# A mixture-of-experts decoder layer on one core: gate and branch products with the tokens on the partitions, merged rows transposed, and 24 unread products in the routing

## The chip, the cores and the metric

The kernel runs on one core of a Trainium2 chip. The time is device microseconds of one execution. Before the change three runs gave 510.54, 511.18 and 512.19 us, with a median of 511.18 us.

## The reference

One layer of a decoder works on 256 tokens of width 1024, all in float32. It has two halves, and a layer norm with a residual closes each. The core of it is:

```
p  = split(x @ w_in)                                   # q, k, v, ... of four mixers, and 4 x 1024 gate columns
ys = stack(mixer_a, mixer_b, mixer_c, mixer_d)         # each (256 tokens, 256)
gates  = sigmoid(p["gate"].reshape(256, 4, 1024))
merged = sum_n gates[:, n] * (ys[:, n] @ w_branch[n])  # (256, 1024)
x = layer_norm(ALPHA * x + merged @ w_out)
# routing: one of 4 groups, then 2 of its 8 experts for each token; then
y = sum over the chosen experts of weight * down(silu(gate(x)) * up(x))
x = layer_norm(ALPHA * x + y)
```

The mixers are A (dilated sliding-window attention), B (attention to the 64 best keys of an indexer), C (chunked gated linear attention) and D (a delta-rule recurrence). There are 32 experts with three matrices of 1 MB each, 96 MB of weights in all.

## The kernel before

**Precision.** Products of the first half are made of three fp32r products: an operand is split into a high part (ScalarE, `A.copy`, line 366) and a low part (VectorE, line 367), and `mm3` (lines 379 to 383) issues low times high, high times low and high times high into one PSUM bank.

**The tiles of w_in.** `TILES` lists 56 tiles of 128x1024 numbers: 24 for the mixers, then for each branch, in the order B, A, C, D, eight gate tiles `gB0` to `gB7` and so on. `gen_S` splits a tile and issues the loads of later ones; `gen_P` makes the products of a tile. A gate tile holds 128 gate columns for all 1024 inputs. Its weights are the stationary operand and the 256 tokens of x the moving one, so that a tile is 8 x 3 products of 256 columns; two tiles fill one of the two PSUM banks of the pool `pj`, and one tanh (line 489) empties it.

**Merging.** `gen_M` does sixteen steps, four to a branch. A step makes 12 products of 256 columns (the branch weights are stationary, the branch's tokens move), then VectorE multiplies by one plus the tanh (line 1182), and from the second branch on GpSimd, or VectorE for the last branch D, adds (line 1185). For D the sum is split into high and low (lines 1192 and 1194). The result lies with the model dimension on the partitions. `gen_N` loads and splits the branch weights, and `gen_U` loads x and splits the output weights. `gen_O` makes merged @ w_out: 96 products of 512 columns, of which the first 48 need only the first half of the merged rows, and the next 48 the second half.

**Routing.** `gen_R(0)` and `gen_R(1)` do a token half each: residual, transposes (line 1367), router logits (line 1384), then a row of small VectorE steps, products with `tri` and `ones` for the ranks (lines 1415 and 1417), and the selection matrix. `gen_E` gathers the tokens of the first four experts (line 1464). `gen_Z` normalises.

**Experts.** Eight groups of four experts follow. `gen_L` starts to fetch their weights once the mixers' memory is given back (`gen_X`); up to 25 pieces of 1 MB are ahead, and each later piece is issued on SP's queue (line 1264) when the products that read its slot are done. 17 slots of the pool `rp` are shared by all that lasts long: loaded and split tiles, gates, merged rows, and the pieces of expert weights.

**The order.** All of this is Python generators, and each `yield` ends a step. The string `ORDER` names, letter by letter, which generator does its next step, so it fixes the order of the instructions on every engine and in SP's queue. Each engine works through its own in order.

Of the kernel before, what the change touches and what calls it, by code (L numbers as in the profile page):

```python
# [9 lines left out]
F32 = mybir.dt.float32  # L10
# [7 lines left out]
P = 128  # L18
# [95 lines left out]
def _layout(inp):  # L114
# [14 lines left out]
    for n in TILES:  # L129
        if n[:2] in ("av", "cv"):  # L130
            o0 = (512 if n[0] == "a" else 1640)
            h = int(n[2])
            cols.append(W[512 * h:512 * h + 512, o0:o0 + 256].reshape(4, P, 256).transpose(1, 0, 2).reshape(P, 1024))
            continue
        if n == "sm":
            c = sm
        elif n == "ck":
            c = ck
        else:
            o0 = 3000 + 1024 * "ABCD".index(n[1]) + 128 * int(n[2]) if n[0] == "g" else at[n[:-1]] + 128 * int(n[-1])  # L140
            c = W[:, o0:o0 + 128]
        cols.append(c.reshape(KT, P, P).transpose(1, 0, 2).reshape(P, 1024))
    o["win"] = np.stack(cols).reshape(len(TILES) // 2, 2, P, 1024).transpose(0, 2, 1, 3)
# [65 lines left out]
SA = 1  # L209

ORDER = (
    "PSBYNDSSFSUSSXSSDPRSSQZPCDOSPEPDDDBSDDDDSPDPPDSDPDDSDPDSPPPFSDFPSPDWAFDDPPDPBSDDPDSDDBBDDDPFDDDDDPDP"
    "SDSWDPDPDBBPPWDSDSBPBBDPDSDBDPCSCDCPBPDDDWDBBMCDDBDDDBWSDSPPBWDDBBSBPDBBDPDDBWDDDDDSDDBDBDBDDBDPBDDP"
    "DBBPDDDSPDDDBDDSPDPBDDDDBDSPDDDDDBDDDDDPNNBNBDDPDDDDDDDDBPAADAANAAAADSDDDDDAASADPPAABDDABABADPBBSAAB"
    "BADADAADDDBBDBAAAAADDBDSDDBDDBBDBBPASBBBBSBBBBDPDBDPBBBCDCPBCCBBBAPSMCMCDCCCCMNCCCPCMCCMSCCCCPPSPPMN"
    "MSPNSMNPSMPSMMPMNCCSPMPSCPDDSPPPCMSSNPMCMSMMLCXPSMLLLLMPLNLNPSMMPSPLPSMMPSMMMPPSNPSPMPSPNSMMLMPPSMMM"
    "PMNPMMLNMPSMSMPMMPMSUUUUUPUMMMMMPPOUULOLLUOSULPMMLMLUUMOLOUUOUUUUOQLOQQQQQQQQQOLLQQQLQQQYYUQQRLQORRQ"
    "RLRRRRQRRRQRRZRQZQERRRRRRRRRLLLREEQQERRE"
)


def body(ctx, tc, I, out):
# [90 lines left out]
    wpart(1, 1)  # L313
    SY.dma_start(pc, I["pc"])
    SY.dma_start(lw, I["lw"])
    load_tiles(2)
    SY.dma_start(cst[:, 0:CC["m2"][0]], I["cst"][:, 0:CC["m2"][0]])
    SY.dma_start(csts, I["cst"][:, NMIX:NCC])
    SY.dma_start(cst[:, CC["m2"][0]:NMIX], I["cst"][:, CC["m2"][0]:NMIX])
    for i in range(4, AHEAD, 2):  # L320
# [108 lines left out]
    def gen_S():  # L429

        yield 0
        first = [(*twin("hl", [P, KT, P], dt=F32R), view(w_sb.pop(i), 1024, [P, KT, P])) for i in range(2)]
        for c in "x0 w00 x1 x2 w01 x3 w10 w11".split():
            if c[0] == "x":
                ks = slice(2 * int(c[1]), 2 * int(c[1]) + 2)
                halves(xh[:, ks], xl[:, ks], xT[:, ks])
            else:
                i, ks = int(c[1]), slice(4 * int(c[2]), 4 * int(c[2]) + 4)
                hi, lo, src = first[i]
                halves(hi[:, ks], lo[:, ks], src[:, ks])  # L440
                sp[i] = hi, lo
            if c in ("x3", "w11"):
                parts["S"] += 1
            yield 0
        nxt = AHEAD
        for i, n in enumerate(TILES):
            if i > 1:
                sh = [P, 4, 256] if n[:2] in ("av", "cv") else [P, KT, P]
                sp[i] = split(view(w_sb.pop(i), 1024, sh), sh)
                parts["S"] = i + 1  # L450
            while nxt < len(TILES) + KT and nxt < i + 1 + (AHEAD if i < 8 else MID if i < TI["av1"] else NEAR):
                if nxt < len(TILES):
                    load_tiles(nxt)
                else:
                    load_out()
                nxt += 2

            yield ("P", i - SA)

    def gen_P():  # L460
        pair = None
        for i, n in enumerate(TILES):
            if n in ("av0", "cv0"):
                continue
            yield ("S", i + 1)
            if n in ("av1", "cv1"):
                p = ps([P, 2, 256], pj)
                for q in range(2):
                    for k in range(KT):
                        h, l = sp[i - 1 + k // 4]  # L470
                        mm3(p[:, q], xp(k, slice(128 * q, 128 * q + 128)), (h[:, k % 4], l[:, k % 4]), k == 0, k == KT - 1)
                yield 0
                evacuate(n, p)
                parts["P"] = i + 1
                continue
            c = int(n[-1]) % 2 if n[-1].isdigit() else 0
            if c == 0:
                pair = ps([P, 2, S], pj)
            h, l = sp.pop(i)
            for k in range(KT):  # L480
                mm3(pair[:, c], (h[:, k], l[:, k]), xp(k), k == 0, k == KT - 1)
            if n[0] == "g":
                m = int(n[2])
                if c:
                    yield 0
                    if m == 1:
                        gslot[n[1]] = slot("g" + n[1], [P, 4, 2, S])
                    gts[n[1], m // 2] = t = gslot[n[1]][:, m // 2]
                    A.activation(t, pair, AF.Tanh, scale=0.5)
                    if i == len(TILES) - 1:  # L490
                        ready(AF.Sqrt, t[:, 1, 0:1])
            else:
                if i == 0:
                    V.tensor_scalar(omm, pc[:, PC["mu"][0]:PC["mu"][0] + 7], -1.0, 1.0, op0=OP.mult, op1=OP.add)
                if n == "ak0":
                    G.memset(into("ak", [P, 2, 2, S]), 0.0)
                yield 0
                evacuate(n, pair[:, c])
            parts["P"] = i + 1


# [658 lines left out]
    def gen_M():  # L1160
        parts["M"] = 0
        for b_, n in enumerate(ORDER_OF_BRANCHES):
            first, final = b_ == 0, b_ == 3
            for jj in range(4):
                i, j2 = jj // 2, slice(2 * (jj % 2), 2 * (jj % 2) + 2)
                yield (n, ("N", 2 * b_ + i + 1))
                h, l = wsp[2 * b_ + i]
                yh, yl = parts[n]
                pbr = ps([P, 2, S])
                for c in range(2):  # L1170
                    cs = slice(256 * (jj % 2) + 128 * c, 256 * (jj % 2) + 128 * c + 128)
                    for k in range(2):
                        mm3(pbr[:, c], (h[:, k, cs], l[:, k, cs]), (yh[:, k], yl[:, k]), k == 0, k == 1)
                parts["M"] += 1
                yield TI[f"g{n}{2 * jj + 1}"] + 1
                g = gts.pop((n, jj))
                if first and jj % 2 == 0:
                    if i == 0:
                        t = slot("mg", [P, 2, 4, S])
                        mg.extend((t[:, 0], t[:, 1]))  # L1180
                dst = mg[i][:, j2]
                V.scalar_tensor_tensor(f2(dst) if first else f2(g), in0=f2(g), scalar=1.0, in1=f2(pbr), op0=OP.add, op1=OP.mult)
                if not first:
                    yield 0
                    (V if final else G).tensor_tensor(dst, dst, g, op=OP.add)
                if final:
                    yield 0
                    if jj == 0:
                        for m in range(2):
                            t = slot("mg" + "hl"[m], [P, 2, 4, S], dt=F32R)  # L1190
                            mgs[m].extend((t[:, 0], t[:, 1]))
                    A.copy(mgs[0][i][:, j2], dst)
                    yield 0
                    V.tensor_tensor(mgs[1][i][:, j2], dst, mgs[0][i][:, j2].bitcast(F32), op=OP.subtract)
                    if jj % 2:
                        parts["mg%d" % i] = True

    def gen_W():

# [144 lines left out]
    def gen_R(q):  # L1344
# [11 lines left out]
        for h in range(2):  # L1356
# [22 lines left out]
                parts["rs%d" % q] = (mv[:, 0:1], rs)  # L1379
            yield 0  # L1380
            if h == 0:
                pl = ps([P, 36])
            for k in range(4 * h, 4 * h + 4):
                T.matmul(pl, lhsT=zT[:, k], rhs=gw[:, k], start=k == 0, stop=k == KT - 1)
        yield 0
        lg = sq_([P, 36], "lg", bufs=2)
        V.scalar_tensor_tensor(lg, in0=pl, scalar=rs, in1=bw, op0=OP.mult, op1=OP.add)

        sm = sq_([P, 8], "smr", bufs=2)
        gm, fm, sg, w1, nv, ex = (sm[:, i:i + 1] for i in range(6))  # L1390
# [20 lines left out]
        V.tensor_scalar(oh[q], le2[:, 0:32], -4.0 * BIG, None, op0=OP.is_equal)  # L1411
        yield "sel0" if q else 0
        if q == 0:
            prks.extend(ps([P, 32]) for _ in range(2))
        T.matmul(prks[q], lhsT=C("tri"), rhs=oh[q], start=q == 0, stop=True)
        if q == 0:
            T.matmul(prks[1], lhsT=C("ones"), rhs=oh[0], start=True, stop=False)
        prk = prks[q]
        yield 0

        rank[q] = sq_([P, 32], "rank%d" % q)
# [52 lines left out]

    XG = {}

    def gen_E():
        yield ("sel0", "nrm0")
        pg = []
# [7 lines left out]
        for kh in range(2):  # L1487
# [3 lines left out]

    gens = {"S": gen_S(), "P": gen_P(), "F": gen_F(), "D": gen_D(), "B": gen_B(), "C": gen_C(), "A": gen_A(), "N": gen_N(),
            "M": gen_M(), "W": gen_W(), "X": gen_X(), "L": gen_L(), "U": gen_U(), "O": gen_O(), "Q": gen_R(0), "R": gen_R(1),
            "Y": gen_Z(0), "Z": gen_Z(1), "E": gen_E()}
    for g in ORDER:
        next(gens[g], None)
    assert all(next(g, None) is None for g in gens.values())
# [283 lines left out]
```

## Time and profile before

| | us |
|---|---|
| profiled execution, its own time | 511.06 |
| span of its instructions | 509.3 |
| TensorE busy | 465.8 (91%) |
| VectorE busy | 239.1 (47%) |
| ScalarE busy | 195.2 (38%) |
| GpSimd busy | 46.5 (9%) |
| mean granted TensorE clock | 0.973 |
| DMA | 146.79 MB, mean 288 GB/s |

A matmul's duration in the profile runs until its result has left the array, and the next one starts long before that. What a product costs in a row of products is therefore the distance between starts, not the duration. A float32 product shows as two records, an fp32r product or a transpose as one. Busy time counts overlapping records once.

### The profile page before, as it was taken

How to read it: one execution, taken by the hardware profiler on the slowest of the kernel's cores; microseconds unless marked ns; L12 is line 12 of the kernel's file. 1: busy time of each engine (PE TensorE's matmuls, PEld its weight loads, DVE VectorE, ACT ScalarE, POOL GpSimd, SP SyncE). 2: the span in 40 equal slices, each digit the busy share in tenths (PEclk: the TensorE clock that was granted, in tenths of full speed). 3: DMA queues.
4: the chain of work that ended last, by engine and by line, in shares of the span. 5: the costliest groups of instructions: out<-in, count | busy, mean ns of one | idle time of the engine just before them, and what ended most of it. 6: DMA issues, size and time to landing. Idle time of an engine off the chain costs nothing. (4 is left out here: it accounts for less than half of the span.)

```text
span 509.3 us, 10326 instructions
## 1 busy us (share of the span) xinstructions
PE 465.8 (91%) x4396; PEld 359.1 (71%) x4396; DVE 239.1 (47%) x479; ACT 195.2 (38%) x357; POOL 46.5 (9%) x55
## 2 busy tenths in 40 slices
PE   7999999999999999999999898998988989877891
PEld 6988888998788999999998676553635446324530
DVE  4577657976877468725665543112211122002015
ACT  5778474355586457424444242001202011101311
POOL 2101111500000011411150000000000000000002
PEclk9999999999999999999999979999999999979897
DMA  8979240340242444699679999999999999999952
GB/s 281 390 309 365 93 161 1 97 155 1 81 169 84 166 166 160 241 423 420 257 291 429 382 399 383 420 349 418 419 417 420 420 423 415 421 420 417 389 190 86
DMA packets 27416, 146.79 MB, mean 288 GB/s; under 512 B 3108, under 2 KB 5736, under 8 KB 12264
## 3 DMA queue, kind: packets, MB, share of 16 engines
q1 hardware_dynamic: 27368, 146.11, 72.8%
q8 instruction: 35, 0.57, 0.4%
q14 instruction: 13, 0.11, 0.1%
HBM read 143.48 MB, written 2.62 MB: 287 GB/s over the span
## 5 line engine op out<-in xcount | busy, mean ns | idle before, releaser
L381 PE MATMUL ps<-xl,hl 128*128 128x256 f32 x416 | 122.9, 295 | 2.3 <-ACT hl L366 1.6
L382 PE MATMUL ps<-xh,hl 128*128 128x256 f32 x416 | 119.0, 286 | 1.3 <-DVE hl L367 1.2
L383 PE MATMUL ps<-xh,hl 128*128 128x256 f32 x416 | 118.6, 285 | 0.0
L367 DVE TENSOR_TENSOR hl<-w,hl 128x1024 fp32r<-128x1024 f32 (+1 forms) x75 | 88.0, 1189 | 51.3 <-ACT hl L366 51.0
L381 PEld LDWEIGHTS ps<-xl,hl 128*128 128x128 f32 x416 | 80.7, 194 | 6.9 <-ACT hl L366 2.2
L382 PEld LDWEIGHTS ps<-xh,hl 128*128 128x128 f32 x416 | 80.7, 194 | 3.3 <-DVE hl L367 2.2
L383 PEld LDWEIGHTS ps<-xh,hl 128*128 128x128 f32 x416 | 80.7, 194 | 0.0
L366 ACT CAST hl<-w 128x1024 fp32r<-128x1024 f32 (+1 forms) x75 | 74.0, 1012 | 14.8 <-DMA w<-win 7.5
L1562 PE MATMUL ps<-w,xg 128*32 128x256 f32 x1024 | 66.6, 402 | 7.5 <-DMA w<-mwu 7.5
L1562 PEld LDWEIGHTS ps<-w,xg 128*32 128x32 f32 x1024 | 33.6, 115 | 38.1 <-DMA w<-mwu 10.1
L1464 PE MATMUL ps<-Sel,nrm 128*128 128x128 f32 x256 | 33.8, 288 | 0.9 <-DVE Sel L1457 0.9
L1464 PEld LDWEIGHTS ps<-Sel,nrm 128*128 128x128 f32 x256 | 31.4, 200 | 4.0 <-issue 3.7
L1549 PE MATMUL ps<-small,SGT 128*128 128x512 f32 x48 | 23.7, 616 | 9.3 <-DVE small L1543 5.1
L1543 DVE COPY small<-ps 128x512 f32<-128x512 f32 x6 | 4.1, 692 | 51.4 <-PE ps L1549 51.4
L1514 ACT COPY SGT<-ps 128x256 f32<-128x256 f32 x8 | 3.0, 372 | 63.3 <-PE ps L1512 63.3
L1531 PE MATMUL ps<-w,small 128*32 128x512 f32 x192 | 23.1, 598 | 3.5 <-ACT xg L1471 3.0
L1549 PEld LDWEIGHTS ps<-small,SGT 128*128 128x128 f32 x48 | 8.2, 189 | 25.0 <-DVE small L1543 10.1
L1704 POOL TENSOR_TENSOR res<-res,ln 128x512 f32<-128x512 f32 x1 | 1.6, 1646 | 235.7 <-ACT res L1703 235.7
L1457 DVE TENSOR_TENSOR Sel<-rank,csts 128x128 f32<-128x128 f32 x16 | 4.0, 289 | 31.2 <-PE ps L1512 31.1
L381 PE MATMUL ps<-parts,hl 128*128 128x256 f32 x64 | 18.6, 291 | 0.0
L382 PE MATMUL ps<-parts,hl 128*128 128x256 f32 x64 | 18.1, 283 | 0.0
L383 PE MATMUL ps<-parts,hl 128*128 128x256 f32 x64 | 18.1, 283 | 0.0
(414 smaller groups left out, 685.2 us busy)
## 6 DMA issues: line engine op xcount, KB each, us to landing
w<-mwu SPq DMA_DIRECT2D x32, 1024.0 KB, 15.0
w<-win SPq DMA_DIRECT2D x27, 1024.0 KB, 6.3
w<-mwg SPq DMA_DIRECT2D x27, 1024.0 KB, 13.6
w<-mwd SPq DMA_DIRECT2D x23, 1024.0 KB, 15.0
w<-mwd SPq DMA_DIRECT2D x10, 512.0 KB, 13.3
w<-mwg SPq DMA_DIRECT2D x10, 512.0 KB, 16.4
w<-wbr SPq DMA_DIRECT2D x4, 1024.0 KB, 5.0
w<-wout SPq DMA_DIRECT2D x4, 1024.0 KB, 6.4
```

What stands on the lines that cost most here:

```text
L366: A.copy(hi, src)
L367: V.tensor_tensor(lo, src, hi.bitcast(F32), op=OP.subtract)
L381: T.matmul(dst, lhsT=ls[0], rhs=rs[1], start=start, stop=False)
L382: T.matmul(dst, lhsT=ls[1], rhs=rs[0], start=False, stop=False)
L383: T.matmul(dst, lhsT=ls[0], rhs=rs[0], start=False, stop=stop)
L1457: V.tensor_tensor(t, rank[q][:, 4 * g:4 * g + 4, None].broadcast_to([P, 4, 32]), C("iota")[:, None, :].broadcast_to([P, 4, 32]), op=OP.is_ ...
L1464: T.matmul(pg[:, k4], lhsT=nrm[q][:, 128 * k:128 * k + 128], rhs=f2(SelR[g, q]), start=q == 0 and k4 == 0, stop=True, skip_group_check=True)
L1514: A.copy(SGT, pg)
L1531: T.matmul(pd[h][32 * e4:32 * e4 + 32], lhsT=outs[g][0][:, k, 32 * e4:32 * e4 + 32], rhs=wds[g][e4](k)[:, 512 * h:512 * h + 512], start=k ...
L1543: V.tensor_copy(dn[h], pd[h])
L1549: T.matmul(yacc[q, h], lhsT=outs[g][1][:, q], rhs=dn[h], start=False, stop=False, skip_group_check=True)
L1562: T.matmul(pgu[32 * e4:32 * e4 + 32, i], lhsT=xg[:, k, 32 * e4:32 * e4 + 32], rhs=ws[e4](k), start=k == 0, stop=k == KT - 1, tile_position ...
```

## The change

1. A gate tile now holds 256 of the 1024 inputs for 512 gate columns (`_layout`), so that four tiles make a half of a branch's gates. x is stationary (128 tokens at a time) and 512 gate columns move. The two token halves fill the two banks of `pj` side by side. Tiles 0 and 1 of a half are used one by one; the third step does nothing, and with the fourth tile both last tiles are used, first for token half 0, whose tanh is then issued, then for token half 1.
2. `gen_M` makes a step for each column half and token half: 6 products of 512 columns. Gates, products and merged rows have the tokens on the partitions. For the last branch four transposes on TensorE bring the sum back to the old layout, and the high and low parts are made from the PSUM bank of the transposes.
3. A new generator `gen_H` issues 24 float32 products of the identity with 64 columns of `tri` into columns 256 to 320 of a bank in use for the routing. Nothing reads them. `parts["spare"]` names the bank, and the router's logits and ranks take a whole bank each for that.
4. Tiles 2 and 3 are loaded in two pieces of 512 KB, with the first piece of constants between them.
5. `ORDER` is a new string with 668 letters instead of 640, among them four more of M and 24 of H.

```
--- before.py
+++ after.py
@@ _layout
+        elif n[0] == "g":
+            o0, k = 3000 + 1024 * "ABCD".index(n[1]) + 512 * (int(n[2]) // 4), 2 * (int(n[2]) % 4)
+            cols.append(W[128 * k:128 * k + 256, o0:o0 + 512].reshape(2, P, 512).transpose(1, 0, 2).reshape(P, 1024))
+            continue
...
@@ ORDER (new; its last three lines)
+    "PSMPSPCSCDPSLDPPCMNPSPMMNPMMPSSMNPMMNPMSPMSPPSCMPPMPXLLLLMSSMPMNNPMLMSLSMMLMPNPMPSSNPPMPMMMPSSMSNMPP"
+    "LSPLPMMMMMMMMSPNMSUUUMPMPPPUUPSMMMMMLLLMMOLMMUMUUOUUMMOUUOOUULLOUUULLUOQOOQQQQQQQQRQLQQOQLQHHLRHQQQR"
+    "RHHHHHHYHQQQRRYRRQURRHHHRHHRQRQHHHHHHRZRQZLRRRRELRRRRLRHHHEQEEQRRELL"
@@ loads
-    load_tiles(2)
+    w_sb[2], w_sb[3] = (lambda t: (t[:, 0], t[:, 1]))(slot("w", [P, 2, 1024]))
+    SY.dma_start(w_sb[2], I["win"][1][:, 0])
     SY.dma_start(cst[:, 0:CC["m2"][0]], I["cst"][:, 0:CC["m2"][0]])
+    SY.dma_start(w_sb[3], I["win"][1][:, 1])
@@ gen_P
+            if n[0] == "g":
+                m, j = int(n[2]) // 4, int(n[2]) % 4
+                if j == 0:
+                    pair = [ps([P, 512], pj) for _ in range(2)]
+                if j != 2:
+                    for q in range(2):
+                        for t in ((i - 1, i) if j == 3 else (i,)):
+                            h, l = sp[t]
+                            for k in range(2):
+                                kk = 2 * (t - i + j) + k
+                                mm3(pair[q], xp(kk, slice(128 * q, 128 * q + 128)), (h[:, k], l[:, k]), kk == 0, kk == KT - 1)
+                        if j == 3:
+                            yield 0
+                            if m == 0 and q == 0:
+                                gslot[n[1]] = slot("g" + n[1], [P, 2, 2, 512])
+                            gts[n[1], m, q] = t = gslot[n[1]][:, m, q]
+                            A.activation(t, pair[q], AF.Tanh, scale=0.5)
...
@@ gen_M
+            for i in range(2):
+                for q in range(2):
+                    yield (n, ("N", 2 * b_ + i + 1))
...
+                    pbr = ps([P, 512])
                     for k in range(2):
-                        mm3(pbr[:, c], (h[:, k, cs], l[:, k, cs]), (yh[:, k], yl[:, k]), k == 0, k == 1)
+                        mm3(pbr, (yh[:, k, ts_], yl[:, k, ts_]), (h[:, k], l[:, k]), k == 0, k == 1)
...
+                        pt = ps([P, 4, P])
+                        for k in range(4):
+                            T.transpose(pt[:, k], dst[:, 128 * k:128 * k + 128], ident)
+                        yield 0
+                        A.copy(mgs[0][i][:, :, ts_], pt)
+                        yield 0
+                        V.tensor_tensor(mgs[1][i][:, :, ts_], pt, mgs[0][i][:, :, ts_].bitcast(F32), op=OP.subtract)
...
+    def gen_H():
+        n = ORDER.count("H")
+        for i in range(n):
+            T.matmul(parts["spare"][:, 256:320], lhsT=ident, rhs=C("tri")[:, 0:64], start=False, stop=True, skip_group_check=True)
+            if i + 1 < n:
+                yield 0
```

## Rows read from the trace of the kernel before

**Rows 1.** Stretches: length; busy us (records) by engine; TensorE clock, DMA share, GB/s.

```profile
225.00:250.00 25.00, 24.13 (x201) 23.93 (x200) 11.68 (x12) 10.62 (x14) 2.59 (x2) 1.00 0.89 368
250.00:264.00 14.00, 14.00 (x119) 14.00 (x118) 9.56 (x10) 5.05 (x7) 6.19 (x7) 1.00 0.79 301
...
325.00:350.00 25.00, 23.55 (x230) 13.32 (x229) 3.79 (x11) 2.63 (x7) 0.00 (x0) 1.00 0.96 379
...
375.00:400.00 25.00, 22.11 (x228) 11.44 (x232) 4.75 (x14) 3.21 (x8) 0.00 (x0) 1.00 1.01 419
```

**Rows 2.** The chain that ended last: start, length, what.

```profile
341.91 1.58 PE ps L1464 x13
343.50 16.88 DMA w<-mwu
...
451.60 19.93 DMA w<-mwu
```

**Rows 3.** Timeline of SP's queue: start, length, DMA issues.

```profile
207.80 2.26 SPq L1264 DMA_DIRECT2D w<-mwg  x4
...
264.12 1.28 SPq L1264 DMA_DIRECT2D w<-mwd  x3
```

**Rows 4.** TensorE's timeline, first and last of 96 products of 256 columns.

```profile
214.78 0.28 PE L381 MATMUL ps<-xl,hl 128*128 128x256 f32 x1
...
226.18 0.28 PE L383 MATMUL ps<-xh,hl 128*128 128x256 f32 x1
```

**Rows 5.** TensorE's timeline: first and last of 84 512-column products; then the routing.

```profile
264.16 0.40 PE L381 MATMUL ps<-hl,mgh 128*128 128x512 f32 x1
...
283.04 0.39 PE L383 MATMUL ps<-hl,mgh 128*128 128x512 f32 x1
...
285.40 0.64 PE L1367 MATMUL ps<-csts,xtok 128*128 128x128 f32 x4
285.79 0.47 PE L381 MATMUL ps<-hl,mgh 128*128 128x512 f32 x1
...
287.95 0.98 PE L1384 MATMUL ps<-gw,zT 128*128 128x36 f32 x8
288.76 0.47 PE L381 MATMUL ps<-hl,mgh 128*128 128x512 f32 x1
```

**Rows 6.** Groups by line and shape: busy us, mean ns; then idle before.

```profile
L366 ACT CAST hl<-w 128x1024 fp32r<-128x1024 f32 x69 | 70.4, 1047 | 13.1 <-PE ps L383 6.7 <-DMA w<-win 6.3
...
L1185 DVE TENSOR_TENSOR mg<-mg,gD 128x512 f32<-128x512 f32 x4 | 2.8, 690 | 0.2
...
L1182 DVE SCALAR_TENSOR_TENSOR gD<-gD,ps 128x512 f32<-128x512 f32 x4 | 2.7, 678 | 0.7 <-ACT eps L347 0.7
...
L489 ACT ACTIVATE gD<-ps 128x512 f32<-128x512 f32 x4 | 2.4, 593 | 2.9 <-PE ps L383 2.9
```

**Rows 7.** Short stretches of the routing, columns as in rows 1.

```profile
292.00:294.50 2.50, 2.25 (x18) 2.02 (x17) 1.83 (x8) 0.91 (x4) 0.00 (x0) 0.85 1.01 423
294.50:296.50 2.00, 1.82 (x9) 1.69 (x9) 0.95 (x5) 1.98 (x2) 0.00 (x0) 0.50 1.00 422
296.50:300.30 3.80, 3.80 (x18) 3.72 (x18) 1.29 (x8) 0.47 (x1) 0.00 (x0) 0.50 0.99 373
300.30:303.00 2.70, 2.00 (x17) 1.86 (x16) 1.25 (x5) 0.00 (x0) 0.00 (x0) 0.95 1.00 413
...
335.00:340.00 5.00, 5.00 (x90) 2.79 (x86) 0.49 (x2) 0.37 (x1) 0.00 (x0) 1.00 0.88 316
340.00:345.00 5.00, 5.00 (x64) 4.07 (x57) 1.90 (x6) 0.76 (x2) 0.00 (x0) 1.00 0.93 326
```

**Rows 8.** Timeline of all engines: the gathers of tokens, and the first expert products.

```profile
296.68 3.41 PE L1464 MATMUL ps<-Sel,nrm 128*128 128x128 f32 x15
...
301.06 2.02 PE L1464 MATMUL ps<-Sel,nrm 128*128 128x128 f32 x16 [0.70 <-DVE Sel L1457]
303.01 3.79 PE L1562 MATMUL ps<-w,xg 128*32 128x256 f32 x64
```

## What the change does to the time, predicted before it was run

> **What bounds the kernel now.** I read the stretches first [rows 1]. From 225 us to the output product, which starts at 264.16 us [rows 5], TensorE has next to no idle time, with VectorE and ScalarE at half of it or less; up to there the kernel is TensorE's row of products. From about 375 us it is the other way round: DMA stands at 1.01 of its time and 419 GB/s, and TensorE waits now and then. The chain that ended last says where one hands over to the other [rows 2]: back to 343.5 us it consists of expert weights on the way, one behind the other, and just before that of the gather at 341.9 us, so of TensorE. The reader should see that the last 160 us have a fixed length (so many MB at 419 GB/s), and that their start is set by TensorE, whose products free the slots for the next weights.
>
> Then I asked whether DMA has room to start earlier, for if not, a faster TensorE buys nothing. It has: between 250 and 264 us it is busy 0.79 of the time at 301 GB/s [rows 1], and three expert pieces leave at 264.12 us [rows 3], just when the last gate product frees their slots. Later there are holes at 335 to 345 us (316 and 326 GB/s where 419 are possible) [rows 7], worth 5 x (103 + 93) / 419 = 2.3 us. So I count a microsecond that TensorE saves before the first expert product (303.01 us, rows 8) as a microsecond at the end.
>
> Last the routing [rows 7]. From about 293.7 to 300.6 us the granted clock is 0.50, the lower level of 1.2 GHz; before it TensorE had only small products with waits between them. The first gather shows the price: 15 records in 3.41 us, where the second, at full clock, has 16 in 2.02 us [rows 8].
>
> **The change part by part.**
>
> *Gate products.* 32 tiles x 24 = 768 products of 256 columns go, 384 of 512 columns come. Ninety-six of the old kind start within 11.40 us, so one each 0.120 us [rows 4]; 84 of the new kind, in the same form (x-like operand stationary, split weights moving), each 18.88 / 83 = 0.2275 us [rows 5]. Two old ones cost 0.240, one new one 0.2275: 384 x 0.0125 = 4.8 us saved. The columns are the same in number; what is saved is a fixed part of about 13 ns for each product. The row bears the sum. The Trainium skill (TensorE: Matmul & The Clock Gate, Part 2, "Back-to-back issue gap") gives a warm product N/2.4 + 2.5 ns, and by that rule a removed product is worth 2.5 ns and both savings of this kind together an estimated 1.2 us. The trace disagrees with it: a product here brings its own weight load, and its fixed part is five times that.
>
> *Branch products.* 16 steps x 12 = 192 products become 96: 96 x 0.0125 = 1.2 us saved. Together 6.0 us.
>
> *Transposes.* Sixteen come. Four took 285.79 - 285.40 = 0.39 us in the routing [rows 5], so 16 cost 1.6 us of TensorE's row.
>
> *A wait in front of the transposes.* TensorE stops at a transpose until VectorE has multiplied and added. In the order written out, the pieces D0, D1 and D3 have gate, branch or output products of 2.7 us or more between the branch product or the gate and the transposes. The third piece has nothing: its branch products are followed at once by its own transposes. They must wait for the tail of the products (0.17 us: 0.395 long, 0.2275 apart), 0.68 and 0.69 us on VectorE [rows 6] and the signals between: 1.7 us. From below it is nothing, if VectorE's row had run ahead, which it can't; from above some 3 us, if VectorE has its half of a split to do first (ScalarE's half takes 1.05 us, rows 6). I take 1.7. Queued behind is the whole output product.
>
> *Bank hand-over.* A bank of `pj` was emptied while the other took 48 x 0.120 = 5.8 us to fill. Now token half 1's tanh ends the half, and the next half writes that bank after six products, 1.36 us. The tanh takes 0.59 us [rows 6] and begins some 0.2 us after the last product, so 0.5 us is left, unless a split (1.05 us, rows 6) is in ScalarE's row before it. There are seven such hand-overs; five have a branch or mixer product in between (1.36 us more). For two, at 0 to 0.7 us each, I take 0.3 us in all: ScalarE is busy 10.62 of 25 us there [rows 1].
>
> *What costs nothing here.* The tanhs, multiplications, additions, splits and loads keep their number and size; the copies from the transposes' bank take the place of the casts of the merged rows, and those of the second half have the first 48 output products, 10.9 us, as cover. If that were gone, it is about 1.4 us once, two operations of the size of those in rows 6. The loads of tiles 2 and 3 can move the first tiles by the time of half a megabyte, 0.5 MB / 419 GB/s = 1.2 us, either way; between the two I take nothing.
>
> *The 24 products.* The nearest row is the router logits: eight records, four products, in 288.76 - 287.95 = 0.81 us [rows 5], 0.2 us a product. In waits they cost nothing; all on the path 24 x 0.2 = 4.9 us, and twice that at half clock. Their use is the clock. The stretch at 1.2 GHz holds some 6.2 us of TensorE work [rows 7]; at 2.4 GHz this is 3.1 us shorter at most (a gain above), and 1.4 us at least (the one gather, rows 8). Following the new order by hand, the unread products stand mainly behind the logits, where the next step waits for VectorE or ScalarE; they hold up the second token half's logits by about 1 us, and the second gather waits for VectorE anyway. I take 2.0 us saved, net.
>
> *Sum,* against the profiled execution's own 511.06 us (509.3 of span and 1.8 around it, 0.12 below the median of the runs): 511.06 - 4.8 - 1.2 + 1.6 + 1.7 + 0.3 - 2.0 = 506.7 us.
>
> **The rivals.**
>
> *The clock falls all the same.* Sixty-four unread columns at a time may not be enough. For it: the transposes and logits of the routing did not hold the clock either. Against: short bursts of output products did, up to 293.7 us [rows 7]. Then the 2.0 us are lost and about half of the unread products, late in the routing, lengthen its slow part by some 1 to 2 us: 506.7 + 2.0 + 1.5 = 510.2 us. The Trainium skill (the same page, Part 4) says that transposes don't count as work for the clock; the rows agree in so far as the stretch with transposes is the one that lost it, and no row separates them from the rest.
>
> *The saving is larger.* TensorE's wait of 0.87 us for VectorE in the stretch from 225 us (24.13 of 25, rows 1) goes with the new order, the transposes' wait is covered, and the clock is worth its full 3.1: 506.7 - 0.9 - 1.7 - 0.3 - 1.1 = 502.7 us.
>
> *The weights don't come earlier.* The first expert pieces leave at 207.8 us [rows 3], once branch C is done and the mixers' memory is free. In the new order that step stands behind 18 gate tiles and 7 branch steps (18 x 2.73 + 7 x 1.37 = 58.7 us) instead of 16 and 8 (16 x 2.88 + 8 x 1.44 = 57.6 us), so a microsecond later, and split tiles are held longer, for the third waits for the fourth. If this sets the stream, the end stays where it is: about 511 us. Against it: DMA's slack before 264 us [rows 1].
>
> *Slower: the hand-over of the banks.* If ScalarE is behind by more than a split at each of the seven hand-overs, TensorE stands still at each. At 0.6 us each the gain is used up (7 x 0.62 = 4.4 us); with 1.3 us each, a split and a bit, the time is 506.7 + 9.1 = 515.8 us. For it: ScalarE works in order, and splits are spread among the tanhs. Against: it is idle for more than half of the stretch.
>
> **How the numbers follow.** The forecast has 0.52 (its own range 504.4 to 509.2), the clock 0.16, the larger saving 0.15, the weights 0.07, the banks 0.10. Predicted: 506.7 us, faster by 0.9%. What a measurement can tell from no change is about 0.3%, 1.5 us: below 509.6 is faster, above 512.7 slower. Faster: 0.52 + 0.15 + a third of the clock's 0.16 = 0.73. Slower: 0.10 for the banks, and 0.03 for the clock with all unread products on the path (506.7 + 2.0 + 4.9 = 513.6) = 0.13. The same: the rest, 0.14. The range from 502.2 to 510.8 leaves out about 0.06 below and 0.14 above.
>
> **What the profile of the changed kernel would show.** Gate products of 512 columns start 0.2275 us apart, and the last gate product ends some 5 us before 264 us. Between the branch products of the third D piece and its transposes stands a wait for VectorE of 1.7 us, and waits at the first product of a gate half stay under 0.7 us. The granted clock stays at 1.00 from the output product to the experts, and both gathers take 2.0 us. The first expert product starts near 298.5 us instead of 303.0 [rows 8]. The chain still ends in a row of expert weights at about 419 GB/s, started 4 us earlier. The prediction is wrong if this row does not move with TensorE, if the clock is 0.50 again, or if TensorE waits for tanhs or splits in the gate stretch for more than 2 us in all.

## The result, and the profile after

The changed kernel takes 504.66 us (median of 4 runs, 503.05 to 505.88) against 511.19 us before (4 runs, 510.54 to 512.19): a ratio of 0.987, 95% interval 0.983 to 0.990. That is faster by 1.3%, where 0.9% and 506.7 us were predicted. It lies at the lower edge of the forecast's own range (504.4 to 509.2), halfway between the forecast and the rival of a larger saving (502.7). The profiled execution took 503.86 us, its span 502.1.

| | before | after |
|---|---|---|
| first output product starts | 264.16 | 258.67 |
| first expert product starts | 303.01 | 297.29 |
| between the two | 38.85 | 38.62 |
| first gather of tokens, from its start to TensorE's next products | 3.57 | 1.84 |
| own time of the execution | 511.06 | 503.86 |

The first gather of before is longer than [rows 8] have it: their 15 records leave out the first one. Whole, it is 16 records in 3.79 us, so full clock is worth 1.77 us in this gather, not 1.4.

```profile
296.31 3.79 PE L1464 MATMUL ps<-Sel,nrm 128*128 128x128 f32 x16 [0.18 <-DVE Sel L1457]
```

Stretches of the profile after, with the columns of [rows 1], busy time in the order TensorE's products, its weight loads, VectorE, ScalarE, GpSimd (they answer to [rows 1, 7]):

```profile
225.00:250.00 25.00, 25.00 (x116) 20.56 (x115) 14.80 (x16) 9.69 (x12) 3.43 (x2) 1.00 0.97 391
258.67:264.00 5.33, 5.33 (x27) 4.41 (x26) 5.17 (x7) 4.51 (x6) 0.00 (x0) 1.00 1.01 423
...
280.00:285.00 5.00, 4.41 (x33) 3.81 (x32) 2.88 (x9) 1.49 (x5) 0.00 (x0) 1.00 0.75 249
285.00:290.00 5.00, 5.00 (x49) 5.00 (x48) 2.55 (x12) 2.72 (x6) 0.00 (x0) 1.00 0.93 390
290.00:295.00 5.00, 4.72 (x43) 4.61 (x43) 2.75 (x17) 2.52 (x2) 0.00 (x0) 1.00 0.78 224
...
335.00:340.00 5.00, 5.00 (x50) 4.02 (x42) 2.21 (x6) 1.46 (x5) 0.00 (x0) 1.00 1.01 419
340.00:345.00 5.00, 3.57 (x30) 0.98 (x27) 0.00 (x0) 1.38 (x4) 0.00 (x0) 1.00 1.01 423
```

The granted clock is 1.00 through the routing, where it had been 0.50 [rows 7]. DMA's holes at 335 to 345 us are closed (419 and 423 GB/s for 316 and 326 in [rows 7]); new ones are at 280 to 285 and 290 to 295 us, where SP's queue waits for the last output products and then, from 284.0 to 290.6 us, for the logits (L1407). Compared with [rows 3], the expert pieces leave 3.4 us earlier, and the three behind the last gate product 10.6 us earlier. About 5 were forecast there; in the new order the last products of branch D stand behind the last gate product.

```profile
204.37 2.20 SPq L1287 DMA_DIRECT2D w<-mwg  x4
...
253.51 1.28 SPq L1287 DMA_DIRECT2D w<-mwd  x3
...
258.87 9.02 SPq L1287 DMA_DIRECT2D w<-mwg  x4
```

The chain that ended last has the shape of [rows 2]: a row of expert weights, and in front of it TensorE, now with the experts' down products.

```profile
340.85 2.90 PE ps L1563 x24
...
344.54 19.68 DMA w<-mwd
364.29 15.26 DMA w<-mwu
...
454.55 15.00 DMA w<-mwd
```

The reader should see that this row begins 1.0 us *later* than before (343.50) though the end is 7.2 us earlier: where the chain changes hands doesn't measure what is still to be moved. By then about 88 MB had been moved (255 GB/s over 344.54 us) against about 85 (247 GB/s over 343.50 us); these 3 MB more are worth some 7 us at 419 GB/s.

TensorE's timeline: the first and the last of 107 products of 512 columns in a row, the wait in front of the third D piece's transposes, the start of the output product, and the routing (L1407 logits, L1440 rank products, L1505 unread products, L1488 gathers, L1594 experts):

```profile
215.80 0.39 PE L388 MATMUL ps<-hl,parts 128*128 128x512 f32 x1
...
239.83 0.39 PE L389 MATMUL ps<-hl,xl 128*128 128x512 f32 x1
...
256.78 0.66 PE L1213 MATMUL ps<-csts,mg 128*128 128x128 f32 x4 [1.72 <-DVE mg L1204]
...
258.67 0.39 PE L388 MATMUL ps<-hl,mgh 128*128 128x512 f32 x1
...
284.50 0.66 PE L1505 MATMUL ps<-csts 128*128 128x64 f32 x4 [0.35 <-DVE lg L1410]
...
285.62 1.67 PE L1505 MATMUL ps<-csts 128*128 128x64 f32 x14
287.13 1.03 PE L1407 MATMUL ps<-gw,zT 128*128 128x36 f32 x8
...
288.47 1.23 PE L1505 MATMUL ps<-csts 128*128 128x64 f32 x10
289.53 1.03 PE L1407 MATMUL ps<-gw,zT 128*128 128x36 f32 x8
...
290.62 0.39 PE L1440 MATMUL ps<-oh,csts 128*128 128x32 f32 x2
290.85 1.53 PE L1505 MATMUL ps<-csts 128*128 128x64 f32 x12
292.21 2.00 PE L1488 MATMUL ps<-Sel,nrm 128*128 128x128 f32 x16
...
294.64 0.88 PE L1505 MATMUL ps<-csts 128*128 128x64 f32 x6 [0.28 <-DVE rank L1446]
295.36 2.00 PE L1488 MATMUL ps<-Sel,nrm 128*128 128x128 f32 x16
297.29 1.93 PE L1594 MATMUL ps<-w,xg 128*32 128x256 f32 x32
```

Between 100 and 264 us the wait of 1.72 us is the only one that TensorE has for another engine. Both gathers take 2.00 us, as forecast. Yet the second half's logits and both gathers start as soon as a block of unread products ends, with no wait in front: so the block is what they stood behind. From the first output to the first expert product the routing became only 0.23 us shorter.

### The profile page after: what moved, and what is told of

The parts are those of the page before. It is cut to its first block, busy times and chain, and to the rows that moved or that the text cites. A ratio compares the mean times of both kernels' runs of the same rounds, so it can differ in the third digit from the quotient of the medians.

```text
span 502.1 us, 9497 instructions
## 1 busy us (share of the span) xinstructions
PE 461.3 (92%) x3980; PEld 336.8 (67%) x3980; DVE 243.3 (48%) x479; ACT 194.9 (39%) x357; POOL 46.8 (9%) x55
## 5 line engine op out<-in xcount | busy, mean ns | idle before, releaser
L374 DVE TENSOR_TENSOR hl<-w,hl 128x1024 fp32r<-128x1024 f32 (+1 forms) x75 | 93.7, 1261 | 35.3 <-ACT hl L373 34.7
L1594 PE MATMUL ps<-w,xg 128*32 128x256 f32 x1024 | 65.9, 400 | 7.5 <-DMA w<-mwu 7.5
L388 PE MATMUL ps<-hl,xh 128*128 128x512 f32 (+1 forms) x160 | 60.8, 380 | 0.0
L390 PE MATMUL ps<-hl,xh 128*128 128x512 f32 (+1 forms) x160 | 58.9, 368 | 0.0
L389 PE MATMUL ps<-hl,xl 128*128 128x512 f32 (+1 forms) x160 | 58.9, 368 | 0.0
L1594 PEld LDWEIGHTS ps<-w,xg 128*32 128x32 f32 x1024 | 33.6, 115 | 37.4 <-DMA w<-mwu 9.9
L388 PE MATMUL ps<-xl,hl 128*128 128x256 f32 x160 | 48.3, 302 | 2.2 <-ACT hl L373 1.6
L389 PE MATMUL ps<-xh,hl 128*128 128x256 f32 x160 | 46.4, 290 | 0.4 <-DVE hl L374 0.3
L390 PE MATMUL ps<-xh,hl 128*128 128x256 f32 x160 | 46.0, 287 | 0.0
L388 PEld LDWEIGHTS ps<-xl,hl 128*128 128x128 f32 x160 | 31.5, 197 | 5.8 <-ACT hl L373 2.2
L388 PEld LDWEIGHTS ps<-hl,xh 128*128 128x128 f32 x160 | 30.1, 188 | 5.8 <-issue 0.7
L389 PEld LDWEIGHTS ps<-hl,xl 128*128 128x128 f32 x160 | 30.2, 189 | 5.3 <-issue 0.5
L390 PEld LDWEIGHTS ps<-hl,xh 128*128 128x128 f32 x160 | 30.1, 188 | 5.1
L389 PEld LDWEIGHTS ps<-xh,hl 128*128 128x128 f32 x160 | 31.6, 198 | 1.2 <-DVE hl L374 0.9
L1488 PE MATMUL ps<-Sel,nrm 128*128 128x128 f32 x256 | 32.0, 278 | 0.0
L1488 PEld LDWEIGHTS ps<-Sel,nrm 128*128 128x128 f32 x256 | 29.8, 192 | 2.9 <-issue 2.9
L390 PEld LDWEIGHTS ps<-xh,hl 128*128 128x128 f32 x160 | 31.5, 197 | 0.0
```

Source lines behind the costliest of these rows:

```text
L374: V.tensor_tensor(lo, src, hi.bitcast(F32), op=OP.subtract)
L388: T.matmul(dst, lhsT=ls[0], rhs=rs[1], start=start, stop=False)
L389: T.matmul(dst, lhsT=ls[1], rhs=rs[0], start=False, stop=False)
L390: T.matmul(dst, lhsT=ls[0], rhs=rs[0], start=False, stop=stop)
L1488: T.matmul(pg[:, k4], lhsT=nrm[q][:, 128 * k:128 * k + 128], rhs=f2(SelR[g, q]), start=q == 0 and k4 == 0, stop=True, skip_group_check=True)
L1594: T.matmul(pgu[32 * e4:32 * e4 + 32, i], lhsT=xg[:, k, 32 * e4:32 * e4 + 32], rhs=ws[e4](k), start=k == 0, stop=k == KT - 1, tile_position ...
```

## The experiments

Times vary by some 1.5 us from run to run, much of it in the first 20 us (last section), so I read three lengths of each profile beside the medians: A, from the first output product to the first expert product (the routing); B, from the issue of the first four gate weights of the experts (`mwg`, [rows 3]) to the first expert product; and C, from TensorE's product of `hot` and `tab` (at 31.98 us before, 31.64 us after, ahead of all that the runs below alter except the first loads) to the first expert product. In A and B the changed kernel repeats to 0.2 us in three profiles, in C to 0.3.

| run | median us (runs) | ratio to before [95%] | A | B | C |
|---|---|---|---|---|---|
| before | 511.19 (4) | | 38.85 | 95.21 | 271.03 |
| after | 504.66 (4) | 0.987 [0.983, 0.990] | 38.62 | 92.92 | 265.65 |
| after_again | 502.99 (6) | 0.984 [0.981, 0.987] | 38.63 | 92.72 | 265.40 |
| after_beside | 505.37 (6) | 0.988 [0.984, 0.991] | 38.62 | 92.72 | 265.43 |
| half_width | 509.97 (12) | 0.998 [0.995, 1.000] | 38.64 | 95.80 | 271.09 |
| half_width_branches | 506.70 (6) | 0.991 [0.988, 0.995] | 38.63 | 93.50 | 266.73 |
| no_unread | 503.39 (6) | 0.985 [0.982, 0.989] | 38.11 | 92.14 | 264.80 |
| ten_unread | 506.32 (11) | 0.989 [0.986, 0.993] | 39.97 | 94.00 | 266.70 |
| double_unread | 510.18 (12) | 1.000 [0.998, 1.002] | 44.00 | 98.03 | 270.73 |
| before_with_unread | 508.37 (12) | 0.998 [0.996, 0.999] | 36.94 | 92.97 | 268.79 |
| loads_together | 504.67 (6) | 0.989 [0.987, 0.992] | 38.64 | 93.05 | 265.75 |
| covered_transposes | 504.64 (6) | 0.987 [0.984, 0.991] | 39.81 | 92.11 | 264.81 |
| fourteen_unread | 502.71 (6) | 0.984 [0.981, 0.987] | 36.59 | 91.04 | 263.77 |
| fourteen_and_cover | 502.42 (6) | 0.982 [0.979, 0.986] | 37.82 | 90.17 | 262.87 |

**after_again** and **after_beside** are the changed kernel, unaltered: the runs were taken in three groups, each on one chip, and these two stand beside the others of the first group (half_width, no_unread, covered_transposes) and of the third (half_width_branches, fourteen_unread, fourteen_and_cover).

> The changed kernel once more, as the measure for the three others on the same chip: 504.7 us, a ratio of 0.987 to the kernel before, by every theory.

> The changed kernel unaltered, as a measure for the other three on the same chip: 503 to 505 by every theory, the first expert product 92.7 to 92.9 us behind the first gate weights' transfer.

**half_width.** Everything stays, but each 512-column product of gates and branches is issued as two of 256.

```
+  for c in range(2):
+      cs = slice(256 * c, 256 * c + 256)
+      T.matmul(dst[:, cs], lhsT=ls[0], rhs=rs[1][:, cs], ...)   # and the other two parts
```

> The changed kernel with each 512-column product of the gates and branches cut into two of 256 columns; layout, transposes, unread products and order stay. Theory (the width saves 0.0125 us for each product that goes, and what TensorE saves ahead of the experts is saved at the end): 480 more products, 6.0 us more, 510.7 us; gate products 0.120 us apart, first expert product 6 us later. Rival (the gain comes from the new order, which took TensorE's waits away, and the width matters little): 504.7 to 506 us.

It takes 7.0 us more than the changed kernel beside it by the medians; the first expert product starts at 302.61 us, 5.3 later than after, and C is 5.4 to 5.7 us longer than in the changed kernel's three profiles. Products are 0.120 us apart again (102 intervals in 12.24 us). The theory holds.

```profile
224.48 0.28 PE L397 MATMUL ps<-hl,parts 128*128 128x256 f32 x1
...
236.72 0.28 PE L397 MATMUL ps<-hl,xh 128*128 128x256 f32 x1
```

All the rest of the change together is worth 1.4 us by the medians of that group (511.34 and 509.97), by the ratio's interval 0 to 2.4; up to the first expert product it is worth nothing (C is 271.09 here and 271.03 before).

**half_width_branches.** The same for the branches' products alone.

> The changed kernel with the branches' products alone in halves of 256 columns, 96 more products; the gates stay 512 wide. Theory (12.5 ns for each product that is saved, wherever it is, as the prediction counts it): 1.2 us of the six that both cost together, the first expert product 93.9 to 94.1 us behind the first gate weights' transfer, the time 1.2 us above the changed kernel's. Rival (the branches' products lie in front of waits for VectorE and ScalarE, which take them up): 92.7 to 93.1 us and no difference in the time, so that all of the width's gain is the gates'.

Measured 1.3 us above after_beside by the medians, the first expert product at 298.37 us, 1.08 later than after; C is 1.1 to 1.3 us longer. B shows less than the whole here (0.8), since some of the branches lie in front of it. The theory holds.

**no_unread.** The 24 steps `H` are taken out of the order, so the products that nothing reads aren't issued.

```
-  ...QLQHHLRHQQQRRHHHHHHYHQQQRRYRRQURRHHHRHHRQRQHHHHHHRZ...ELRRRRLRHHHEQ...
+  ...QLQLRQQQRRYQQQRRYRRQURRRRQRQRZ...ELRRRRLREQ...
```

> The changed kernel without the 24 unread products, all else the same. Theory (they hold the clock, and some 2 us of them lie on the path): the granted clock falls to 0.50 for some 3 to 7 us of the routing, the first gather takes 3.4 us or more, and the first expert product comes 0 to 2 us later: 504.7 to 506.7 us. Rival (the new order holds the clock without them): clock 1.00, first expert product some 2.4 us earlier: 502.3 us.

The clock falls, and the time is the same. Stretches, then TensorE's timeline:

```profile
284.00:288.00 4.00, 3.37 (x17) 2.88 (x17) 2.13 (x9) 1.78 (x4) 0.00 (x0) 0.63 1.00 422
288.00:292.00 4.00, 3.82 (x19) 3.69 (x19) 2.09 (x13) 2.52 (x2) 0.00 (x0) 0.51 0.73 266
```

```profile
288.82 3.50 PE L1488 MATMUL ps<-Sel,nrm 128*128 128x128 f32 x16 [0.18 <-DVE Sel L1481]
...
293.17 2.02 PE L1488 MATMUL ps<-Sel,nrm 128*128 128x128 f32 x16 [0.70 <-DVE smr L1452]
```

The slow gather costs 1.5 us more, and A is still 0.5 us shorter, C 0.6 to 0.9: the unread products give the clock, and in this order they take back more than the gain. The theory is right on the clock and misses the rest: the first expert product was to come 0 to 2 us later.

**ten_unread.** Only `H0` to `H9` stay.

> Only the first ten of the 24 unread products stay; the fourteen ahead of the second half's ranks and of the two gathers go. Theory (the unread products keep the clock, and cost on the path what they give): from the first expert product's side it is a wash; without the twelve records ahead of the first gather (1.53 us from 290.85 us) it can start when the selection is ready, 0.7 us earlier, and if the clock is still 1.00 both gathers stay at 2.0 us, so the first expert product comes 0.7 to 1.1 us earlier and the time is 502.0 to 502.5 against the changed kernel's 503.0. Rival one (the last fourteen are what holds the clock through the gathers): a gather takes 3.4 us and the first expert product comes 0.5 to 1 us later, 503.5 to 504. Rival two (the first expert product doesn't set the end to a microsecond): the time is the changed kernel's within 0.5 us either way, whatever the gathers do.

A miss for the theory, and worse than rival one's gather alone: A grows by 1.35 us. Ten products only put the fall off, to where it hurts, and both gathers run at the lower clock:

```profile
290.24 0.39 PE L1440 MATMUL ps<-oh,csts 128*128 128x32 f32 x2
...
291.14 3.16 PE L1488 MATMUL ps<-Sel,nrm 128*128 128x128 f32 x16 [0.52 <-DVE Sel L1481]
...
295.27 3.65 PE L1488 MATMUL ps<-Sel,nrm 128*128 128x128 f32 x16 [0.70 <-DVE smr L1452]
```

**double_unread.** Each step `H` issues two unread products.

> Each of the 24 places issues two unread products instead of one. Theory (TensorE works them off one behind another at full clock, and they stand ahead of the logits and the gathers): 48 more records of about 0.11 us, of which the waits that are left (0.35 and 0.28 us) take little, so the first expert product comes 4 to 5 us later, at 301 to 302 us, and the time is 507 to 508. Rival (the routing's chain on VectorE is what sets the first expert product, and the products lie beside it): it comes less than 2 us later and the time is 503 to 505.

A grows by 5.38 us for 48 more records, 0.112 us each: every added one is on the path. The theory holds; the median is 4.8 to 7.2 us above the changed kernel's three.

**before_with_unread.** The kernel before with 17 unread products in its own order, and whole banks for them.

```
+ H x5 behind the last output product, x2 and x2 ahead of logits, x4 ahead of each gather
-  pl = ps([P, 36])
+  pl = parts["spare"] = ps([P, 512])
```

> The kernel before, with seventeen unread products of the same form put into its own waits of the routing (five behind the last output product, two and two ahead of logits, four ahead of each gather) and the whole banks that they need. Theory (keeping the clock gives about what the unread products cost on the path): granted clock 1.00 through 294 to 303 us, gathers of 2.0 us in place of 3.4 and 2.0, and the first expert product 0 to 0.6 us earlier: 510.7 to 511.3. Rival one (the prediction's term: 2.0 us net): the first expert product at 301.0, the time 509.2. Rival two (the clock falls all the same): the products only stand in the way, the time 511.5 to 513.

```profile
290.00:295.00 5.00, 4.90 (x45) 4.87 (x44) 4.04 (x17) 3.20 (x8) 0.00 (x0) 1.00 0.99 388
295.00:300.40 5.40, 5.12 (x45) 4.90 (x44) 2.48 (x13) 1.27 (x1) 0.00 (x0) 1.00 0.96 366
```

My theory was too low: A is 1.91 us shorter, which is rival one, the prediction's own term. By the ratio it is 1.3 us (0.4 to 2.1). This is net of what the products cost, for here too the first gather starts at the end of a block with no wait in front:

```profile
293.96 0.39 PE L1417 MATMUL ps<-oh,csts 128*128 128x32 f32 x2
294.19 1.08 PE L1482 MATMUL ps<-csts 128*128 128x64 f32 x8
295.11 2.00 PE L1465 MATMUL ps<-Sel,nrm 128*128 128x128 f32 x16
```

**loads_together.** The second pair of weight tiles is loaded ahead of the constants again.

```
-    SY.dma_start(w_sb[2], ...)   # constants between
-    SY.dma_start(w_sb[3], ...)
+    load_tiles(2)
```

> The changed kernel with the second pair of weight tiles loaded ahead of the constants again, as in the kernel before. Theory (it is nothing by the end): within 0.5 us of the changed kernel, 502.5 to 503.5, and the start of the output products, 258.7 us, moves by less than 0.3 us. Rival (the constants' earlier part is what brought some of the 3.3 us by which the first gate weights' transfers come earlier): the first of these transfers comes 1 us later or more, and the time is 504 to 506.

The median lies among the changed kernel's three (502.99 to 505.37). In the profile the first output product starts 0.98 us later than after, and TensorE is busy 0.7 us less in the first 10 us; but two executions of the unaltered kernel differ by 2.1 us in the start of that product. What this part is worth, between nothing and 1 us, stays open.

**covered_transposes.** The third D piece's branch products are issued ahead of the last twelve gate products, so that its products cover VectorE's work.

```
-  ...PPUUPSMMMM...
+  ...PMPMMUUPSM...
```

> The changed kernel with the order altered at one place: the branch products of the third D piece are issued ahead of the last twelve gate products, so that these cover VectorE's work before the transposes. Theory (TensorE's row sets the end): the wait of 1.72 us goes, first expert product 1.7 us earlier, 503.0 us. Rival (weights on the way already set the end): wait gone, time the same, 504.7 us.

The wait of 1.72 us goes and two others come, the second for a split of the output weight, which VectorE now does later:

```profile
258.79 0.63 PE L1213 MATMUL ps<-csts,mg 128*128 128x128 f32 x4 [0.35 <-DVE mg L1204]
259.83 0.50 PE L388 MATMUL ps<-hl,mgh 128*128 128x512 f32 x1 [0.42 <-DVE hl L374]
```

B falls by 0.6 to 0.8 us and C as much, where the theory had 1.7; the time doesn't show it. (A is no measure here, since the first output product moves ahead.)

**fourteen_unread.** The blocks are thinned where they stand before logits or a gather (7 to 4, 5 to 3, 6 to 3, 3 to 1), 14 of 24 in all.

> The changed kernel with 14 of the 24 unread products, thinned in each place where they stand in front of logits or a gather that would have been ready sooner (7 to 4, 5 to 3, 6 to 3, 3 to 1). Theory (the 24 keep the clock, but those that outlast a wait stand in the way): granted clock 1.00 through the routing, both gathers 2.0 us, the first expert product 1.5 to 2 us sooner behind the first gate weights' transfer, 91.0 to 91.3 us, and the time 1.5 us below the changed kernel's. Rival one (the gaps that open bring the clock down as they do with ten): one or both gathers at 3.2 us or more, and 93 to 94 us. Rival two (the routing's chain on VectorE and ScalarE sets the pace at full clock): 92.3 to 92.7 us, no difference in the time.

```profile
288.00:293.40 5.40, 5.12 (x44) 4.87 (x43) 3.20 (x19) 3.31 (x6) 0.00 (x0) 1.00 0.86 252
```

```profile
287.73 0.39 PE L1440 MATMUL ps<-oh,csts 128*128 128x32 f32 x2
287.95 0.86 PE L1505 MATMUL ps<-csts 128*128 128x64 f32 x6
288.65 2.03 PE L1488 MATMUL ps<-Sel,nrm 128*128 128x128 f32 x16
...
291.10 0.43 PE L1505 MATMUL ps<-csts 128*128 128x64 f32 x2 [0.28 <-DVE rank L1446]
291.52 2.02 PE L1488 MATMUL ps<-Sel,nrm 128*128 128x128 f32 x16
```

The theory holds: clock 1.00, both gathers 2.0 us, A 2.03 us shorter (20 records x 0.11 = 2.2). The six runs lie between 501.25 and 503.71 us, those of after_beside between 503.45 and 506.72; the medians differ by 2.7 us, more than A or C (1.6 to 1.9) explains.

How long a block may be can be read from the rank products (L1440) in front of the first gather. With nothing between, the gather starts 0.90 us behind their start (ten_unread: 290.24 to 291.14), and VectorE sets that. With six records it starts 0.92 us behind (287.73 to 288.65), with twelve 1.59 us (after: 290.62 to 292.21). So six records lie in the wait, and the other six stand in the way.

**fourteen_and_cover.** Both edits.

> The same, and the products of the third piece of branch D issued ahead of the last twelve gate products as well. Theory (two savings that add): 0.6 us less than with fourteen unread products alone, 90.4 to 90.7 us, if those hold the clock; the time 2 us below the changed kernel's. Rival (a microsecond off TensorE's path no longer brings the end forward, since the expert weights' transfers wait for free buffers): the first expert product comes sooner by that and the time is within 0.7 us of the changed kernel's.

B is another 0.87 us shorter, the median 0.3 us: the two savings add up to the first expert product; at the end the second can't be told from nothing. This kernel has the lowest median here; its runs, 500.55 to 503.21 us, are below every run of after_beside.

## Why the prediction was right, and where two errors met

- **What sets the end.** Right: the first expert product came 5.72 us earlier and the execution's own time 7.2 us. The sign that was named for it, the last row of expert weights starting 4 us earlier, failed as worded, since another piece heads the row; what moved is the amount already fetched by then, the 3 MB above. The extra 1.5 us are not shown to have one cause. The sum had not counted DMA's holes at 335 to 345 us, and they closed; but in before_with_unread they nearly close too (395 and 421 GB/s), and there the stretch from the first expert product to the end of the span is 205.8 us against 206.3 before. In the changed kernel's three profiles that stretch is 204.4 to 205.7 us, so 0.6 to 1.9 us shorter.
- **Width.** Right in mechanism, 6.0 us predicted: 5.3 measured by half_width's first expert product, 5.4 to 5.7 by C, 7.0 by the medians; 1.1 to 1.3 of it the branches' (1.2 predicted). The new products are 0.227 us apart (106 intervals in 24.03 us from 215.80 us). The Trainium skill (TensorE: Matmul & The Clock Gate, Part 2, "Back-to-back issue gap") also states 131 ns for 512 columns in a stream with weight loads; no two of these products came nearer than 0.22 us in the profile after, so for this kernel the measured spacing holds.
- **The wait in front of the third D piece's transposes.** Right: 1.72 us against 1.7 (1.51 and 1.54 in after_again and after_beside). Taking it away is worth less than the wait, 0.6 to 0.8 us, for VectorE has other work due at that place.
- **Bank hand-over.** Taken at 0.3 us; none shows. The slower rival didn't come.
- **What failed: the 24 products, 2.0 us net.** "In waits they cost nothing" is borne out: the six records that fourteen_unread leaves in front of the first gather cost 0.02 us. In the order of before, seventeen products give 1.91 us net. But in the changed kernel too many of them outlast the waits. "They hold up the second token half's logits by about 1 us, and the second gather waits for VectorE anyway" put the hold-up at half of what it is, and left out the first gather: thinning them gave 2.03 us. The 2.0 us counted for the products came to a loss of 0.5: A is 38.62 us with them and 38.11 without (no_unread). That A is still 0.23 us shorter than before, about 0.6 without the four transposes that now lie in it, comes from the rest of the change.
- **What made up for it: the stretch up to the output product.** The prediction's terms for it (4.8 + 1.2, less 1.2 for 12 of the 16 transposes, less 1.7 and 0.3) come to 2.8 us; 5.49 were measured. Two waits of before that the sum left standing are gone, 0.87 us from 225 us [rows 1] (the prediction had it only in a rival) and 0.86 us between 130 and 150 us, and the hand-over's 0.3. That is 2.0 of the 2.7 us, less 0.4 for the width (5.6 for 6.0). Another 0.3 lie ahead of the product of `hot` and `tab`, where the starting loads and the first 20 us of an execution can't be told apart. The remaining 0.7 us no run takes apart.

So 506.7 - 2.7 (up to the output product) + 1.4 (routing: 0.2 for 2.0 less the 0.4 of its transposes) - 1.5 (behind the first expert product) = 503.9 us, the profiled execution's own time. The routing was put 1.4 us too good and the other two parts 4.2 us too bad; that the forecast is 2.8 us off and not 4.2 is luck, for errors of both signs met.

## What to carry to other kernels

Filler products that keep TensorE's clock paid here as far as each block was no longer than the wait it lay in: count the records in a block (0.11 us each here) against the time at which the next real operand is ready, which a run without the block shows, and thin the block to that. Fillers that stop short of the costly products were worse than none (ten_unread, A 39.97 us for 38.11), because the fall of the clock was put off into those products. And when a reordered kernel is forecast, list the waits of the old order that lie in the rebuilt stretch as a term of the sum, not only as a rival.

## What the hardware showed that was not expected

The clock in the first 20 us differs between executions of one and the same kernel, and all that follows is shifted. TensorE's stretch from 10 us in after_again, in after_beside and in fourteen_unread (the same code up to the output product):

```profile
10.00:15.00 5.00, 4.74 (x28) 4.74 (x29) 3.01 (x10) 2.91 (x6) 0.00 (x0) 0.66 1.04 415
```

```profile
10.00:15.00 5.00, 4.40 (x19) 4.13 (x20) 3.68 (x10) 2.75 (x6) 0.00 (x0) 0.50 1.03 412
```

```profile
10.00:15.00 5.00, 5.00 (x39) 4.84 (x39) 2.89 (x10) 2.94 (x7) 0.00 (x0) 1.00 1.05 415
```

The first `mwg` issue follows at 204.46, 206.56 and 202.43 us. That is 4.1 us between the first and the last of the three, as much as many edits; lengths inside a profile compare kernels better than single times. Why the clock differs stays open.
